# Token tile 0 first at the changes of phase, convolution inputs in 512-wide blocks, other stretches in the first feed-forward front

## The chip, the core and the metric

The kernel runs on one core of a Trainium2 chip. The metric is the device time of one execution in microseconds (us); a lower one is better. Engines are named as in the profile: PE (TensorE matmuls), PEld (its weight loads), DVE (VectorE), ACT (ScalarE), POOL (GpSimd), SP (SyncE, which issues all loads here).

## What is computed

One layer of a streaming encoder on 256 tokens of width 2048, in float32:

```python
h = modulate(rms_norm(x, g_pre[0]), sh1, sc1)
x = x + 0.5 * gt1 * rms_norm(swiglu(h, gate1, up1, down1), g_post[0])   # 5632 wide

h = modulate(rms_norm(x, g_pre[1]), sh2, sc2)
u_conv, q, k, v = split(h @ w_in)                   # 2 x 1024, 1024, 1024, 1024
v_c = (a + b_a) * sigmoid(g + b_g)                  # a, g: the halves of u_conv
y_conv = silu(layer_norm(causal depthwise conv of 31 taps(v_c) + b_dw))
y_attn = diff_attention(q, k, v)                    # 8 heads, chunk-causal, ALiBi
x = x + gt2 * rms_norm(concat(y_conv, y_attn) @ w_out, g_post[1])

h = modulate(rms_norm(x, g_pre[2]), sh3, sc3)
x = x + 0.5 * gt3 * rms_norm(swiglu(h, gate2, up2, down2), g_post[2])
```

The nine rows sh, sc, gt come from `silu(c) @ w_ada`, an 18432 x 2048 matrix that is read in 144 loads of 1 MB, one per row set m (0 to 8) and channel tile kt (0 to 15).

## The kernel before

**Products.** Each float32 product is made of three matmuls (`mm3`, lines 272 to 274): every operand is split in a high part that the PE takes at full rate and a low rest. `parts` (156 to 168) loads 1 MB of weights into one of 4 `raw` buffers, ACT casts it to `hi` (line 160), DVE subtracts to get `lo` (line 162); `hi` and `lo` have 3 buffers each. Weights that run through the array against 128 tokens give tiles of 128 tokens x 512 outputs ("M form": `m_product`, 24 matmuls of 512 columns for 1 MB). `s_tile` and the class `Front` hold the weights in the array and run 256 tokens through ("S form": 48 matmuls of 256 columns for 1 MB, result with channels on the partitions).

**Phases.** There are three: feed-forward 0, mixing, feed-forward 1 (l = 0, 1, 2). Each begins with `pre_norm`, which for each of the 16 channel tiles transposes the normalised rows of both token tiles on the PE (line 218), scales and shifts them on ACT or DVE (225, 222) and splits them (227, 228). `front_of` (558) does so two tiles ahead of the first block of products: for l = 1 the S form with 2 channel tiles of the convolution (`NF`, `SET`: 4 MB of weights), for l = 2 three M blocks (12 MB). The remaining convolution inputs, 12 MB, go through `s_tile`.

**End of a phase.** `m_last` (418) makes the last two output blocks token tile by token tile, so that `close` (253) of tile 0 runs while tile 1 is multiplied. `close` and `normed` add the residual (line 260), sum the squares (236), take a root and scale (247 on DVE, 245 on ACT). The gate is multiplied in place after the squares (line 489).

**The first front.** For l = 0 the h tiles become ready one by one, since each needs two chunks of w_ada (`ada_chunk`, line 183). `first_front` (518) therefore runs 4 fronts of 3 blocks in 4 stretches of 4 channel tiles (`CUTS`), and spills the sums between the stretches (lines 354, 358). Within a stretch the tiles of the next one are made.

**Chunks in the background.** 96 chunks of w_ada (m = 2 to 7) are drawn from the generator `bg`: in the last stretch of the first front, then one per 1.1 loads in the first feed-forward (`EVERY1`; 80 calls of `tick`), 8 in the mixing, the rest in the front of l = 2. They share the `raw` buffers and the SP queue with the weights; in the front of l = 2 their DVE work stands behind the newest `pre_norm` (`behind_dve`).

**Convolution.** When a pair of channel tiles is ready, its 62 taps (`tap`, lines 627 and 630, DVE) go to the list `fill`; each later call of `parts` puts 6 of them behind its own `lo`. What is left when half of the second `of_heads` block is done is issued at once by `conv_done` (832), and `center`, `normalize` and the products `of_conv` follow.

**Order.** A scheduler places the instructions of each engine by program order and by its own estimate of when they can run; the engines take them in that fixed order. `behind` and `behind_dve` set a lower bound for some. PSUM has 8 banks.

## Time and profile before

| | us |
|---|---|
| median of 3 runs (lowest, highest) | 1912.85 (1911.74, 1914.44) |
| the profiled execution | 1911.84 |
| its span in the trace | 1910.0 |
| PE busy in the span | 1836.3 (96%) |
| DVE busy | 1423.6 (75%) |
| ACT busy | 821.4 (43%) |
| moved by DMA | 492.58 MB, mean 258 GB/s |

A matmul's record overlaps the next one, and its end is modelled. So the busy share of the PE tells where it had nothing at all, and the distance of two starts, or the count in a stretch, tells what a matmul costs. "Idle before, <- X" names what ended the wait.

### The profile page before, as it was taken

The page shows a single profiled execution, that of the slowest core. Times are in us where ns is not written, and L with a number is a line of the kernel's source. Part 1 is how long each engine was busy: PE and PEld are TensorE (multiplying, and loading weights), DVE is VectorE, ACT ScalarE, POOL GpSimd, SP SyncE. Part 2 cuts the span into 40 slices and gives each one's busy share as a digit, 9 for nine tenths or more (in the row PEclk, how much of TensorE's full clock was granted, in tenths as well). Part 3 has the DMA queues.
Part 4 walks back from the last instruction along what each step waited for, and adds up shares of the span by engine and source line. Part 5 has one row for each costly group of instructions (what it writes and reads, how often), then busy time and mean ns, then how long its engine had stood idle before and what let it go on. Part 6 is the DMA issues. An engine that isn't in the chain of part 4 may idle for free.

```text
span 1910.0 us, 22064 instructions
## 1 busy us (share of the span) xinstructions
PE 1836.3 (96%) x8944; PEld 1542.5 (81%) x8944; DVE 1423.6 (75%) x1594; ACT 821.4 (43%) x852; POOL 6.0 (0%) x49
## 2 busy tenths in 40 slices
PE   5999999999999999799998897999999999999997
PEld 3788888888888888699997686788888888888886
DVE  7789999788889888688998967854555555555455
ACT  4544445433433334643554454544344333343342
POOL 0000000000000000000000000000000000000000
PEclk9999999999999999899999898999999999999999
DMA  9888877989999998355444665865665666565552
GB/s 362 320 317 330 337 278 290 358 345 361 357 357 370 349 367 323 122 182 185 157 174 157 242 241 202 331 238 205 236 220 205 235 220 226 215 235 210 194 193 72
DMA packets 68934, 492.58 MB, mean 258 GB/s; under 512 B 7648, under 2 KB 7776, under 8 KB 9440
## 3 DMA queue, kind: packets, MB, share of 16 engines
q1 hardware_dynamic: 68832, 491.17, 69.0%
q8 instruction: 70, 1.15, 0.2%
q14 instruction: 32, 0.26, 0.0%
HBM read 489.05 MB, written 2.10 MB: 257 GB/s over the span
## 4 chain that ended last, share of the span: by engine, by line
PE 89%; DVE 5%; ACT 3%; DMA 2%; issue 0%; SPq 0%; DVEq 0%; ACTq 0%
PE ps L273 29%; PE ps L274 29%; PE ps L272 28%; DVE lo L162 2%; DMA raw<-in_wgu 2%; ACT hi L160 1%; DVE raw L183 1%; PE ps L413 1%; ACT tmp L236 1%; PE ps L312 0%; PE ps L311 0%; DMA raw<-in_wk 0%; PE ps L313 0%; PE ps L678 0%; PE ps L218 0%
## 5 line engine op out<-in xcount | busy, mean ns | idle before, releaser
L162 DVE TENSOR_TENSOR lo<-raw,hi 128x2048 fp32r<-128x2048 f32 x314 | 718.5, 2290 | 359.8 <-ACT hi L160 359.1
L160 ACT CAST hi<-raw 128x2048 fp32r<-128x2048 f32 x314 | 600.3, 1912 | 732.4 <-PE ps L274 362.0
L272 PE MATMUL ps<-hi,big 128*128 128x512 f32 x2256 | 879.2, 395 | 16.9 <-ACT big L227 11.3
L273 PE MATMUL ps<-lo,big 128*128 128x512 f32 x2256 | 884.0, 392 | 2.8 <-DVE lo L162 2.8
L274 PE MATMUL ps<-hi,big 128*128 128x512 f32 x2256 | 881.5, 392 | 2.0 <-DVE big L175 1.2
L272 PEld LDWEIGHTS ps<-hi,big 128*128 128x128 f32 x2256 | 426.1, 189 | 106.4 <-ACT big L227 12.7
L273 PEld LDWEIGHTS ps<-lo,big 128*128 128x128 f32 x2256 | 426.5, 189 | 92.5 <-DVE lo L162 6.2
L274 PEld LDWEIGHTS ps<-hi,big 128*128 128x128 f32 x2256 | 425.7, 189 | 92.5 <-DVE big L175 2.5
L183 DVE SCALAR_TENSOR_TENSOR raw<-raw,crow 128x2048 f32<-128x2048 f32 x144 | 327.7, 2283 | 0.6 <-DMA raw<-in_wada 0.5
L272 PE MATMUL ps<-big,hi 128*128 128x256 f32 x448 | 127.3, 284 | 0.0
L273 PE MATMUL ps<-big,hi 128*128 128x256 f32 x448 | 126.7, 283 | 0.0
L274 PE MATMUL ps<-big,lo 128*128 128x256 f32 x448 | 126.7, 283 | 0.0
L630 DVE SCALAR_TENSOR_TENSOR big<-big,par,big 128x256 f32<-128x256 f32 x240 | 100.1, 477 | 0.0
L272 PEld LDWEIGHTS ps<-big,hi 128*128 128x128 f32 x448 | 85.9, 192 | 0.3 <-issue 0.3
L273 PEld LDWEIGHTS ps<-big,hi 128*128 128x128 f32 x448 | 86.0, 192 | 0.0
L274 PEld LDWEIGHTS ps<-big,lo 128*128 128x128 f32 x448 | 85.9, 192 | 0.0
L397 ACT ACTIVATE tmp<-ps 128x256 f32<-128x256 f32 x64 | 24.3, 384 | 96.3 <-PE ps L274 96.3
L486 DVE TENSOR_TENSOR big<-ps,big 128x512 f32<-128x512 f32 x48 | 32.9, 691 | 31.7 <-PE ps L274 31.7
L358 DVE TENSOR_TENSOR big<-ps,big 128x512 f32<-128x512 f32 x72 | 45.2, 681 | 5.4 <-PE ps L274 5.4
L398 DVE TENSOR_TENSOR tmp<-ps,tmp 128x256 f32<-128x256 f32 x64 | 26.1, 421 | 30.9 <-ACT tmp L397 30.9
L218 PE MATMUL ps<-ident,big 128*128 128x128 f32 x96 | 19.7, 297 | 29.6 <-DVE big L247 28.7
L173 ACT CAST big<-ps 128x512 fp32r<-128x512 f32 x44 | 25.8, 585 | 38.0 <-PE ps L413 38.0
(135 smaller groups left out, 742.6 us busy)
## 6 DMA issues: line engine op xcount, KB each, us to landing
raw<-in_wada SPq DMA_DIRECT2D x144, 1024.0 KB, 6.1
raw<-in_wgu SPq DMA_DIRECT2D x116, 1024.0 KB, 5.0
raw<-in_wd SPq DMA_DIRECT2D x88, 1024.0 KB, 5.0
raw<-in_wk SPq DMA_DIRECT2D x60, 1024.0 KB, 5.5
raw<-in_wqk SPq DMA_DIRECT2D x28, 1024.0 KB, 4.8
raw<-in_wo SPq DMA_DIRECT2D x16, 1024.0 KB, 4.8
raw<-in_wv SPq DMA_DIRECT2D x8, 1024.0 KB, 4.8
raw<-in_wkc SPq DMA_DIRECT2D x4, 1024.0 KB, 5.1
```

Source lines behind the costliest of these rows:

```text
L160: nc.scalar.copy(hi, raw)
L162: ins = nc.vector.tensor_tensor(out=lo, in0=raw, in1=hi.bitcast(F32), op=ALU.subtract)
L173: nc.scalar.copy(hi[:, :w], v[:, :w])
L183: nc.vector.scalar_tensor_tensor(out=raw, in0=raw, scalar=1.0, in1=crow, op0=ALU.mult, op1=ALU.mult, accum_out=acc)
L272: nc.tensor.matmul(o, ah, bh, start=first, stop=False)
L273: nc.tensor.matmul(o, ah, bl, start=False, stop=False)
L274: last_mm[0] = nc.tensor.matmul(o, al, bh, start=False, stop=last)
L358: nc.vector.tensor_tensor(out=a[t], in0=b[t], in1=a[t], op=ALU.add)
L397: nc.scalar.activation(v[:, o], b[t][:, :S], AF.Silu)
L398: nc.vector.tensor_tensor(out=v[:, o], in0=b[t][:, S:], in1=v[:, o], op=ALU.mult)
L486: nc.vector.tensor_tensor(out=y[t][u], in0=b, in1=y[t][u], op=ALU.add)
L630: nc.vector.scalar_tensor_tensor(out=cot(c), in0=vps[c][:, j:j + S], scalar=w, in1=cot(c), op0=ALU.mult, op1=ALU.add)
```

## The change

Four things are changed.

1. `Entry` takes the place of `front_of`. Its list of items goes over the first k0 = 12/n channel tiles (n blocks: 6 tiles for l = 1, 4 for l = 2) with token tile 0 alone, then over the same tiles with token tile 1, then over the rest with both. Two items (`LEAD`) are made inside `m_last`, `EARLY` = 3 steps before its last product. `pre_norm` takes the token tiles as an argument, and the gate is multiplied into a new tile (`yg`).
2. The convolution inputs are in M form: a front of 2 blocks (8 MB) and two `m_unit` of 4 MB. `gated` transposes the result back (8 transposes a block) and appends the taps; it is called through `left`, that is by a `pop` in a later unit.
3. `CUTS` is (2, 6, 11, 16): stretches of 2, 4, 5 and 5 channel tiles. A stretch of 2 has 6 weight blocks per front, loaded as 4 and 2 (1 MB and 0.5 MB); one of 5 has 15, loaded as 4, 4, 4, 3. There are 52 loads where there were 48, of the same 48 MB.
4. `EVERY1` is 1.05. The setup of lambda and of the distances stands ahead of the first feed-forward in the program.

```diff
-NF = (24, 2, 6)
+NF = (24, 4, 6)
-SET = (6, 2, 6)
-CUTS = (4, 8, 12, NK)
-EVERY1 = 1.1
+SET = (6, 4, 6)
+CUTS = (2, 6, 11, NK)
+EVERY1 = 1.05
+EARLY = 3
@@ pre_norm
-    def pre_norm(l, xn, h, kt):
+    def pre_norm(l, xn, h, kt, ts=(0, 1)):
-        for t in range(NT):
+        for t in ts:
@@ m_last
+                    if t == NT - 1 and u == units[-1][0] and k == n - EARLY:
+                        early()
                     m_product(banks[u][t], t, acts[k], ws[u][k], first[u] and k == 0, k == n - 1)
@@ ffn, evac
-                    nc.vector.tensor_tensor(out=y[t][u], in0=y[t][u], in1=gb[u], op=ALU.mult)
+                    yg = big()
+                    nc.vector.tensor_tensor(out=yg, in0=y[t][u], in1=gb[u], op=ALU.mult)
+                    y[t][u] = yg
@@ front_of
-        for i in range(NK + LEAD):
-            if i < NK:
-                need([(3 * l, i), (3 * l + 1, i)], late)
-                pre_norm(l, xn, h, i)
-            n_late += 1
-            while n_late >= LATE:
-                n_late -= LATE
-                behind_dve(next, late, None)
-            if i >= LEAD:
-                front.step(i - LEAD, i == LEAD, i == NK + LEAD - 1)
+    class Entry:
+            k0 = 4 * HI // self.front.n
+            self.items = [(kt, (t,)) for t in range(NT) for kt in range(k0)]
+            self.items += [(kt, (0, 1)) for kt in range(k0, NK)]
+        def early(self, xn):
+            for _ in range(LEAD):
+                behind(self.channels, xn)
+        def run(self, xn):
+            n_late = 0
+            for kt, ts in self.items:
+                self.channels(xn)
+                n_late += len(ts) / 2
+                while n_late >= LATE:
+                    n_late -= LATE
+                    behind_dve(next, self.late, None)
+                self.front.step(kt, kt == 0, kt == NK - 1, ts)
@@ convolution inputs
-            ba = s_tile(wqk[c - NF[1]], h)
-            bgg = s_tile(wqk[NC_ - 2 * NF[1] + c], h)
...
-        if c % 2:
-            fill += [lambda c=c_, j=j: tap(c, j) for j in range(KW) for c_ in (c - 1, c)]
+    def gated(cb, us):
+        ba, bg_ = bank(), bank()
+        for half, b in enumerate((ba, bg_)):
+            for j in range(2):
+                for t in range(NT):
+                    nc.tensor.transpose(b[:, j * S + t * P:j * S + (t + 1) * P],
+                                        us[t][:, half * S + j * P:half * S + (j + 1) * P], ident)
...
+        fill.extend([lambda c=c_, j=j: tap(c, j) for j in range(KW) for c_ in (2 * cb, 2 * cb + 1)])
+    def conv_block(cb, banks):
...
+        left.append(lambda: behind(gated, cb, us))
+    for cb in range(NC_ // 2):
+        if cb < front.n:
+            conv_block(cb, front.block(cb))
+        else:
+            conv_block(cb, m_unit([wcv[kq, cb] for kq in range(4)], hacts))
@@ heads
         project(w_q, hd, 0)
+        pop()
```

## Rows read from the trace of the kernel before

**Rows 1.** The page's head.
```profile
span 1910.0 us, 22064 instructions
```

**Rows 2.** Waits of PE: line, releaser, us in total, times, longest.
```profile
PE ps L218 <- DVE big L247: 28.7, 5, 10.9
```

**Rows 3.** Busy time by stretch, PE alone: bounds, length, busy (instructions), clock, DMA share, GB/s.
```profile
20.60:51.50 30.90, 23.10 (x74) 0.89 0.94 359
51.50:102.40 50.90, 49.55 (x222) 1.00 0.87 331
...
500.00:550.00 50.00, 49.22 (x219) 1.00 0.96 356
...
774.00:819.00 45.00, 32.59 (x238) 0.81 0.32 114
830.00:850.00 20.00, 20.00 (x169) 1.00 0.57 203
...
1084.00:1098.00 14.00, 7.73 (x26) 0.63 0.75 283
1149.70:1170.00 20.30, 8.60 (x34) 0.66 0.43 153
```

**Rows 4.** The page's groups of instructions: count, busy us, mean ns of one, idle before.
```profile
L272 PE MATMUL ps<-hi,big 128*128 128x512 f32 x2256 | 879.2, 395 | 16.9 <-ACT big L227 11.3
...
L272 PE MATMUL ps<-big,hi 128*128 128x256 f32 x448 | 127.3, 284 | 0.0
```

**Rows 5.** Timeline of PE at 1014 and 1035 us: start, length, operation.
```profile
1014.75 0.39 PE L272 MATMUL ps<-hi,big 128*128 128x512 f32 x1
1014.98 0.39 PE L273 MATMUL ps<-lo,big 128*128 128x512 f32 x1
...
1035.81 1.03 PE L760 MATMUL ps<-ident,tmp 128*128 128x128 f32 x8
```

**Rows 6.** Timeline around the change of phase to the mixing, DVE and PE.
```profile
769.29 2.73 DVE L260 SCALAR_TENSOR_TENSOR x<-big,ri,x 128x512 f32<-128x512 f32 x4
...
779.90 0.88 DVE L247 TENSOR_SCALAR big<-x,ri 128x512 f32<-128x512 f32 x2
...
785.90 0.88 DVE L247 TENSOR_SCALAR big<-x,ri 128x512 f32<-128x512 f32 x2
...
788.14 0.79 PE L311 MATMUL ps<-big,hi 128*128 128x256 f32 x2 [0.79 <-ACT big L227]
```

**Rows 7.** The same around the change of phase to feed-forward 1, DVE and SP.
```profile
1146.23 0.88 DVE L247 TENSOR_SCALAR big<-x,ri 128x512 f32<-128x512 f32 x2
...
1160.87 0.88 DVE L247 TENSOR_SCALAR big<-x,ri 128x512 f32<-128x512 f32 x2
...
1163.77 2.28 DVE L183 SCALAR_TENSOR_TENSOR raw<-raw,crow 128x2048 f32<-128x2048 f32 x1
...
1151.76 0.33 SPq L153 DMA_DIRECT2D raw<-in_wk  x1
```

**Rows 8.** Timeline of ACT at the start: first and fourth cast of weights.
```profile
17.49 1.90 ACT L160 CAST hi<-raw 128x2048 fp32r<-128x2048 f32 x1 [2.22 <-DMA raw<-in_wk]
...
46.29 1.89 ACT L160 CAST hi<-raw 128x2048 fp32r<-128x2048 f32 x1
```

**Rows 9.** Timeline of DVE and PE from the last taps to the first convolution product.
```profile
1055.63 2.06 DVE L630 SCALAR_TENSOR_TENSOR big<-big,par,big 128x256 f32<-128x256 f32 x5
1057.61 0.68 DVE L789 TENSOR_TENSOR tmp<-big,big 128x512 f32<-128x512 f32 x1
1058.22 2.28 DVE L183 SCALAR_TENSOR_TENSOR raw<-raw,crow 128x2048 f32<-128x2048 f32 x1
...
1079.53 2.28 DVE L183 SCALAR_TENSOR_TENSOR raw<-raw,crow 128x2048 f32<-128x2048 f32 x1
...
1090.73 0.80 PE L272 MATMUL ps<-hi,big 128*128 128x512 f32 x1 [3.43 <-ACT big L173]
```

**Rows 10.** DMA issues: count, KB each, median us to landing.
```profile
raw<-in_wk SPq DMA_DIRECT2D x60, 1024.0 KB, 5.5
...
x<-in_x SPq DMA_DIRECT2D x4, 512.0 KB, 6.0
```

More of the change, by code (lines that the diff above doesn't have):

```diff
@@ L48, with chunks @@
 FF_GROUPS = [(0, 12), (12, 24), (24, 36), (36, 44)]
-NF = (24, 2, 6)
+NF = (24, 4, 6)
 HM, HC, HV = 4, 3, 2
-SET = (6, 2, 6)
-CUTS = (4, 8, 12, NK)
-EVERY1 = 1.1
+SET = (6, 4, 6)
+CUTS = (2, 6, 11, NK)
+def chunks(l):
+    n = SET[l] // 2
+    r = []
+    for k0, k1 in zip((0,) + CUTS, CUTS) if l == 0 else ((0, NK),):
+        r += [(i, min(i + 4, k1 * n)) for i in range(k0 * n, k1 * n, 4)]
+    return r
+EVERY1 = 1.05
 TAPS = (3, 3, 3, 3)
@@ L218, in pre_norm @@
             nc.tensor.transpose(b[:, t * P:(t + 1) * P], src[:, o:o + P], ident)
+        if len(h) == kt:
+            h.append(big(F32R))
+        both = h[kt]
+        o, e = ts[0] * P, (ts[-1] + 1) * P
         v = tmp()
@@ L342, in step @@
                 i = kt * n + j
-                if i % 4 == 0:
-                    self.parts = quarters(self.w[i // 4])
-                for t in range(NT):
-                    m_product(self.banks[j][t], t, (self.h[kt][:, :S], self.h[kt][:, S:]), self.parts[i % 4],
-                              first, last)
+                c, i0, i1 = self.chunk[i]
+                if c not in self.parts:
+                    self.parts[c] = quarters(self.w[c], i1 - i0)
+                for t in ts:
+                    m_product(self.banks[j][t], t, (self.h[kt][:, :S], self.h[kt][:, S:]),
+                              self.parts[c][i - i0], first, last)
         def spill(self):
@@ L416, in to_acts, with m_last @@
         acts.extend([(mh[:, o:o + S], ml[:, o:o + S]) for o in (0, S)])
-    def m_last(units, acts, after):
+    def m_last(units, acts, after, early=lambda: None):
         ws, first = {}, {}
@@ L502, in ffn @@
                     gb[u] = gate_row(l, u)
-                m_last([(u, srcs(u), None) for u in range(4 - N_LAST, 4)], acts, evac)
+                m_last([(u, srcs(u), None) for u in range(4 - N_LAST, 4)], acts, evac,
+                       (lambda: nxt.early(xn)) if nxt else (lambda: None))
         return xn
@@ L521, in first_front @@
         h = []
-        front = [MFront(w, h, SET[0] // 2) for w in wk]
+        front = [Front(0, w, h) for w in wk]
         def channels(kt):
@@ L612, in block_kernel @@
     nc.vector.tensor_scalar(out=nlam, in0=nlam, scalar1=-LAM_INIT, scalar2=None, op0=ALU.add)
-    h = []
+    mixing = Entry(1, wkc[0], bg)
+    xn = ffn(0, h, None, facts, wgu1, wd1, bg, EVERY1, mixing)
     need([(m, kt) for m in (3, 4) for kt in range(NK)], bg)
-    h, front = front_of(1, xn, wkc[0], iter(()))
+    mixing.late = iter(())
+    h, front = mixing.run(xn)
     co = [big() for _ in range(NC_ // 2)]
@@ L718, in values @@
     def values(u, hooks):
-        hacts = [(h[kt][:, :S], h[kt][:, S:]) for kt in range(NK)]
         banks = m_unit([wv[kq, u] for kq in range(4)], hacts, hooks)
@@ L842, in block_kernel @@
     gb = {}
+    second = Entry(2, wk2[0], bg)
     def mix_evac(u, t, b):
@@ L861, in block_kernel @@
                 mix_evac(u, t, open_[u][t])
-    m_last([(u, of_conv(u), open_[u]) for u in range(4 - N_LAST, 4)], conv_acts, mix_evac)
-    h, front = front_of(2, xn, wk2[0], bg)
-    ffn(2, h, front, {}, wgu2, wd2, ada_of([(8, kt) for kt in range(NK)]), 6, True)
+    m_last([(u, of_conv(u), open_[u]) for u in range(4 - N_LAST, 4)], conv_acts, mix_evac,
+           lambda: second.early(xn))
+    h, front = second.run(xn)
+    ffn(2, h, front, {}, wgu2, wd2, ada_of([(8, kt) for kt in range(NK)]), 6, None)
 def _layout(i):
```

152 lines of the change are left out of this document (65 added, 87 removed).

## The prediction

> **What bounds the kernel now.** I read the head of the page first [rows 1]: the span is 1910.0 us, the profiled execution took 1911.84 us, so 1.84 us lie outside the span, and the median of the runs is 1.0 us above that execution. My sum is made against 1911.84.
>
> Next I asked what a matmul costs. The page's groups give a mean of 395 ns for 512 columns and 284 ns for 256 [rows 4]. Those are lengths of overlapping records. Two starts in a dense stretch are 0.227 us apart [rows 5], and 169 matmuls of 256 columns fill 20.0 us [rows 3], so 0.118 us each. I use these two steps. The PE is the engine that sets the time almost everywhere, and what a change can win is either fewer steps or the stretches where the PE has nothing. The stretches by time show four such places [rows 3], and the list of waits names the largest cause: transposes of `pre_norm` that wait for `normed`, 28.7 us in five waits [rows 2].
>
> - Start: from 20.6 to 51.5 us there are 74 matmuls, which are worth 74 x 0.227 = 16.8 us. So by 51.5 us 51.5 - 16.8 = 34.7 us are lost, and DMA is at 0.94. From 51.5 to 102.4 us, 222 x 0.227 = 50.4 of 50.9 us are used.
> - Entry to the mixing, 774 to 819 us: 238 instructions, of which 32 are transposes. A group of 8 transposes takes 1.03 us [rows 5], so 0.13 each. The rest is worth 206 x 0.118 + 32 x 0.13 = 28.5 us. The loss is 16.5 us. The mean clock is 0.81.
> - Entry to feed-forward 1, 1149.7 to 1170 us: 28 x 0.227 + 6 x 0.13 = 7.1 of 20.3 us. The loss is 13.2 us.
> - First convolution products, 1084 to 1098 us: 26 instructions at clock 0.63, so at least 14 - 26 x 0.227 = 8.1 us are lost.
>
> **The change part by part.** *Token tile 0 first.* Six channel tiles x 2 blocks x 3 matmuls, and four x 3 x 3, are 36 matmuls of tile 0 in each entry, 36 x 0.227 = 8.2 us of work that no longer waits for tile 1. In the entry to the mixing `normed` of tile 0 starts at 779.9 and that of tile 1 at 785.9 [rows 6]. From `normed` to the first product it is 788.1 - 785.9 = 2.2 us. With these times tile 0 could begin at 782.1 and fill 6.0 us. But tile 0 is late here: from its `close` at 769.3 to its `normed` are 10.6 us [rows 6], since splits of weights and steps of tile 1 stand between on DVE and ACT. The new tile `yg` takes one wait out of that chain. If tile 0 is ready when the last product ends (about 774 us), all 8.2 us fit. The PE also stays at the upper of its two clock levels for longer: mean 0.81 over 45 us is 17 us at half, of which about 12 are idle, so 5 us of work run at half the pace and cost 2.5 us. Against this stand the two early `pre_norm`: their transposes sit in the PE's fixed order ahead of 9 products of the old phase. If `normed` of tile 0 comes at 779.9 as before, those 9 products and the chain of tile 1 behind them wait up to 6 us. Range of the gain 2 to 10.7; I take 7.
>
> In the entry to feed-forward 1, `normed` of tile 0 starts at 1146.2, ahead of the last product, and that of tile 1 at 1160.9 [rows 7]. So the early transposes hold nothing back. Here the weights could: the third chunk of the front is issued only at 1151.8, because three chunks of w_ada hold `raw` buffers until their DVE step, the first at 1163.8 [rows 7]. In the new order only one chunk of w_ada stands ahead of that load (`n_late` counts halves), so the load moves forward into the old phase and ACT and DVE can split it as soon as `hi` is free. Gain 8.2 us and part of the clock loss, less 1 to 2 us by which the extra halves of `pre_norm` hold up the chain of tile 1. Range 4 to 11; I take 9.
>
> *Convolution inputs in M form.* 16 MB change form: 48 x 0.118 = 5.68 us each before, 24 x 0.227 = 5.44 us after, so 16 x 0.24 = 3.8 us less. The way back costs 32 transposes, 32 x 0.13 = 4.1 us. Together 0. (The mean lengths would have given 16 x (48 x 0.284 - 24 x 0.395) = 66 us, which is not there.) The Trainium skill, "TensorE: Matmul & The Clock Gate", section "Back-to-back issue gap", puts a matmul at N/2.4 + 2.5 ns, 109 ns for 256 columns and 216 ns for 512. By that, an estimate, the form would win only 16 x (5.24 - 5.18) = 1 us and lose 3 us with the transposes. The rows differ from it by 9 and 11 ns, and I go by the rows.
>
> *Taps.* This is the price of the new form. Before, `fill` has entries after the first pair, and 12 convolution loads, 16 of q and k, 8 of v and 4 of the heads take 6 each: 240 of 248 taps, and 8 are left for `conv_done`. After, the front's 8 loads take none, since `gated` comes only with the `pop` in the next unit, after that unit's first load. So 3 + 4 + 16 + 8 + 4 = 35 loads take 210 taps and 38 are left. Five taps and the step to the next operation take 1.98 us [rows 9], 0.396 each, so 30 more are 11.9 us of DVE between the last load and `center`. The first convolution product hangs on that chain: last tap to 1057.6, `center` from there, product at 1090.7 [rows 9], and the PE waits for it. Not all of 11.9 us need show. Between 1058.2 and 1079.5 four passes over w_ada, 2.28 us each [rows 9], stand in the chain's gaps, 9.1 us that can come later. Upward, two `lo` of the next unit, which read as many elements (2 x 2.3), and these passes may end up ahead of the chain: 11.9 + 4.6 + 9.1 = 25. Range 3 to 25. I take 8, nearer the lower end, since `center` finished well before its sum on the PE was due.
>
> *Stretches.* In the first stretch 6 channels (12 loads of w_ada) and 6 MB of weights are moved, 18 MB. The stretch to 51.5 us moved 359 GB/s, 2.92 us for 1 MB [rows 3]. The third load was cast at 17.5 us and the twelfth at 46.3 [rows 8], 3.2 us each. At 3.0 us the last one is there at 17.4 + 15 x 3.0 = 62.4, and with 2.4 us for its split and 2.7 us for its 12 products the stretch ends at 67.5 us. Its products are 4 x 6 x 2 x 3 x 0.227 = 32.7 us, so 34.8 us are lost, where before 34.7 were lost at 51.5 us. The first h comes no sooner in either. So 0. Bounds: loads of 0.5 MB may cost as much as whole ones (512 KB landed in 6.0 us, 1024 KB in 5.5 [rows 10]); four of them at 1.5 us extra are +6. If the two chunks of the last channel come after the weights of the stretch, it ends 2 x 3.0 us sooner, less a little that the next stretch waits: -5. Later stretches are set by the PE.
>
> *Background.* 80 calls at 1.05 give 76 chunks instead of 72, and the last front stretch gives 6 instead of 5. So feed-forward 0 moves 4 MB more, 11.7 us of DMA time where DMA is at 0.96 and 0.8 us of 50 are idle [rows 3]. As the PE was just covered there, I take +1.5, up to +8. The front of l = 2 moves 5 MB less: 6 instead of 11 chunks, -1 (0 to -1.5). The split of `pre_norm` adds no PE work. `yg`, the earlier setup, the odd loads of 0.75 MB lie beside products: 0, and if uncovered one load's 3 us.
>
> Sum: -7 - 9 + 0 + 8 + 0 + 1.5 - 1 = -7.5, so 1911.84 - 7.5 = 1904.3 us. I forecast 1904.
>
> **Rivals.**
> - *The tail of taps is absorbed.* The scheduler puts the passes over w_ada behind the chain, 11.9 - 9.1 = 3, and both entries give their full amounts: -10 - 10 + 3 + 0.5 = -16.5, 1895 us. For it: PE idles in the chain anyway. Against: the PE takes the two sums of the layer norm at fixed places.
> - *Tile 0 does not lead.* `normed` of tile 0 comes as late as before and the early transposes block the PE: 2 + 4 won, 8 lost, 0.5: +2.5, 1914 us, no change that can be measured. For it: 779.9 against 774 in the first entry. Against: 1146.2 against 1149.7 in the second.
> - *The tail of taps takes over the stage.* At `conv_done`, 38 taps stand ahead of `center` and of the next `lo`, and the chain comes the full 25 us late: -16 + 25 + 0.5 = +9.5, 1921 us. It turns the sign once the first convolution product comes more than about 20 us later against the end of the old phase than the 316 us of now (774 to 1090). For it: 30 taps are certain by the count. Against: half of the 25 us are passes that nothing needs yet.
>
> **How the numbers follow.** Forecast (1897 to 1909) 0.48, absorbed tail 0.18, no lead 0.18, tail takes over 0.16. About 0.2%, 3.8 us, is what a measurement of this kernel can tell from no change, so "same" is 1909.0 to 1916.7. Faster 0.48 + 0.18 = 0.66, same 0.18, slower 0.16. The range takes in the absorbed tail with the better bound of the start (1890) and reaches towards the taking over of the tail (1918): 1889 to 1918.
>
> **What would show it.** In the trace after, tile 0's products should start within 3 us of the last product of the old phase, and the 28.7 us of waits on `normed` should fall under 12. The convolution loads should be 24 matmuls 0.227 apart. About 38 taps should stand between the last `lo` ahead of `conv_done` and `center`, which begins some 12 us later against that `lo`. The clock should stay up through the entries. 5 loads fewer of w_ada should lie in the front of l = 2. I would be wrong if the early transposes show as a PE wait in front of the last 9 products, if the PE waits in the last 20 us of the mixing grow by over 15 us, or if the start loses over 40 us.

## The result: slower by 1.1%

| | us |
|---|---|
| median before, 4 runs beside the changed kernel | 1913.14 (1911.74 to 1914.44) |
| median after, 4 runs | 1934.17 (1931.64 to 1934.83) |
| ratio, 95% interval | 1.0108 (1.0090 to 1.0125) |
| profiled execution after, its span | 1931.64, 1929.8 |
| forecast, range | 1904, 1889 to 1918 |

The forecast had the wrong sign and the time lies above its range. The head of the page after, the line of PE, and the shares of the engines on the chain that ended last (PE had 89% of that chain before, DVE 5%, DMA 2%):

```profile
span 1929.8 us, 21442 instructions
...
PE 1843.6 (96%) x8592; PEld 1524.7 (79%) x8592; DVE 1425.5 (74%) x1613; ACT 828.5 (43%) x879; POOL 6.0 (0%) x49
...
PE 77%; DVE 11%; DMA 7%; ACT 4%; issue 1%; SPq 0%; DVEq 0%; ACTq 0%
```

PE still has 96%, and that share says nothing: what changed is how much of the chain goes through the other engines.

**Where the time went.** I followed the PE through both traces by the distance from each matmul's start to the next, less what a matmul costs in a dense stretch (0.2267 us for 512 columns, 0.1183 for 256, 0.109 for a transpose). What is left over is a loss, whatever its cause, a low clock included. The work, counted at these steps, is the same in both kernels, 1803.1 us before and 1802.8 after. The losses from the first to the last matmul are 92.8 and 113.9 us, 21.1 more, against 19.8 us more of span. Their places, in us, for all kernels of this study (times without a number of runs are one run each):

| | start, to 150 us | FF 0, 150 to 700 | its end | entry 1 | mixing | tail of the convolution | entry 2 | front of l = 2 | from 1880 us | time (runs) |
|---|---|---|---|---|---|---|---|---|---|---|
| before | 31.8 | 3.2 | 0.2 | 17.0 | 3.6 | 20.1 | 14.2 | 2.0 | 0.0 | 1913.14 (4) |
| after | 39.9 | 8.8 | 4.6 | 12.8 | 2.7 | 32.5 | 9.9 | 0.5 | 1.5 | 1934.17 (4) |
| e1 | 33.9 | 7.7 | 4.6 | 12.9 | 2.6 | 28.4 | 8.9 | 3.2 | 1.5 | 1921.83 |
| e2 | 42.5 | 5.8 | 2.7 | 15.2 | 2.6 | 32.3 | 9.8 | 4.7 | 1.5 | 1935.59 |
| e3 | 42.1 | 9.3 | 4.9 | 15.5 | 3.6 | 16.9 | 8.9 | 1.1 | 1.5 | 1922.25 |
| e4 | 43.3 | 8.2 | 4.7 | 16.3 | 2.6 | 32.6 | 14.8 | 0.4 | 1.6 | 1943.00 |
| e5 | 32.5 | 8.0 | 0.2 | 16.4 | 3.7 | 29.4 | 14.4 | 2.7 | 0.0 | 1927.12 |
| e6 | 32.5 | 3.2 | 3.4 | 15.5 | 3.4 | 21.4 | 9.7 | 7.2 | 1.5 | 1914.48 (12) |
| e7 | 33.3 | 6.2 | 3.9 | 12.8 | 3.5 | 21.3 | 9.4 | 3.2 | 1.5 | 1917.39 (12) |
| e8 | 44.3 | 9.4 | 4.1 | 15.4 | 2.7 | 32.4 | 9.8 | 0.7 | 1.6 | 1938.84 |
| e9 | 34.2 | 2.3 | 0.3 | 14.1 | 3.4 | 21.1 | 9.7 | 6.6 | 0.0 | 1910.55 (11) |
| e11 | 37.2 | 15.7 | 6.7 | 12.8 | 2.7 | 32.4 | 9.9 | 0.5 | 1.6 | 1937.77 |
| e12 | 38.8 | 5.8 | 0.3 | 14.8 | 3.4 | 16.9 | 9.0 | 16.2 | 0.0 | 1925.79 (4) |
| e13 | 35.2 | 4.4 | 0.2 | 14.9 | 3.5 | 21.2 | 9.6 | 3.2 | 0.0 | 1912.92 (11) |

The entries are counted from 12 us (l = 1) or 4 us (l = 2) ahead of their first transposes to 32 and 36 us behind them, the tail 45 us to both sides of the first sum of the layer norm. Each row is one trace. Kernels with the same program up to 150 us (after, e2, e3, e4) differ by up to 3.4 us there. The kernel before and e5 run the same instructions in the same order up to 819 us, and lose 3.2 and 8.0 us in feed-forward 0. The changed kernel and e3 do so up to 861 us, and lose 12.8 and 15.5 us in entry 1. So a single difference of 3 us in the first column or in entry 1, or of 5 us in feed-forward 0, says little.

Four places got worse: the start by 8.1, the first feed-forward with its end by 10.0, the tail of the convolution by 12.4, the end of the kernel by 1.5. The entries got better by 4.2 and 4.3.

**The tail, after.** Waits of PE between 1040 and 1130 us (line, releaser, us in total, times, longest), then what the DVE does ahead of the first sum:

```profile
PE ps L806 <- DVE tmp L814: 11.4, 1, 11.4
PE ps L286 <- ACT big L185: 5.3, 1, 5.3
```

```profile
1066.52 2.27 DVE L174 TENSOR_TENSOR lo<-raw,hi 128x2048 fp32r<-128x2048 f32 x1
1068.72 17.50 DVE L633 SCALAR_TENSOR_TENSOR big<-big,par,big 128x256 f32<-128x256 f32 x44
1086.15 0.67 DVE L812 TENSOR_TENSOR tmp<-big,big 128x512 f32<-128x512 f32 x1
1086.76 2.27 DVE L174 TENSOR_TENSOR lo<-raw,hi 128x2048 fp32r<-128x2048 f32 x1
1088.96 0.67 DVE L814 TENSOR_TENSOR tmp<-tmp,big 128x512 f32<-128x512 f32 x1
1089.56 2.27 DVE L174 TENSOR_TENSOR lo<-raw,hi 128x2048 fp32r<-128x2048 f32 x1
1091.76 0.67 DVE L814 TENSOR_TENSOR tmp<-tmp,big 128x512 f32<-128x512 f32 x1
...
1094.57 2.27 DVE L195 SCALAR_TENSOR_TENSOR raw<-raw,crow 128x2048 f32<-128x2048 f32 x1
```

44 taps stand in one block: the last 6 that `parts` takes and the 38 that are left. `center` (line 812) comes behind them, where before it came right behind 5 taps [rows 9]. Two `lo` got in between its additions, which end at 1092.4 us, and the first sum on the PE waits 11.4 us for that. Two passes over w_ada (the second at 1094.57) come behind the additions, ahead of the subtractions of `center`. Before, the additions ended at 1061.8 us and the sum started at 1068.5 without a wait, so there were 6.7 us of room. Against the PE's own work the additions now end 18 us later: 11.9 us are the 30 taps. Most of the rest are three `lo` of 2.27 us ahead of and between the additions, where before one pass over w_ada of 2.28 us stood.

**The end of the first feed-forward, after.** ACT, PE and SP around 767 us, in this order:

```profile
766.11 0.63 ACT L250 ACTIVATE tmp<-big 128x512 f32<-128x512 f32 x1 [8.57 <-DVE big L467]
...
767.41 1.64 ACT L185 CAST big<-raw 128x512 fp32r<-128x512 f32 x3
...
768.07 0.50 PE L286 MATMUL ps<-big,big 128*128 128x512 f32 x1 [2.04 <-ACT big L185]
...
753.21 10.00 SPq L165 DMA_DIRECT2D raw<-in_wd  x4
773.21 0.93 SPq L165 DMA_DIRECT2D raw<-in_wkc  x2
```

The casts of the second-last block's weights into `big` tiles (line 185) begin at 767.41 us, although those weights were issued from 753.21 us on. In ACT's fixed order they stand behind the squares of the block before (line 250), for which ACT has waited 8.57 us. The PE waits for the first cast. The loads of the convolution inputs (`in_wkc`) need the `raw` buffers and are issued only at 773.21 us, when the subtraction behind the first casts (line 187) is done.

**The start, after.** Busy time by stretch (bounds, length, PE, PEld, DVE, ACT, POOL, clock, DMA share, GB/s), and DVE in the middle of the second stretch:

```profile
60.00:80.00 20.00, 15.32 (x64) 11.61 (x65) 15.33 (x13) 12.55 (x17) 0.00 (x0) 1.00 0.79 303
110.00:130.00 20.00, 17.18 (x78) 13.76 (x77) 20.00 (x24) 10.51 (x9) 0.00 (x0) 1.00 0.89 347
```

```profile
118.55 2.29 DVE L195 SCALAR_TENSOR_TENSOR raw<-raw,crow 128x2048 f32<-128x2048 f32 x1
...
120.76 2.29 DVE L195 SCALAR_TENSOR_TENSOR raw<-raw,crow 128x2048 f32<-128x2048 f32 x1
...
122.97 3.72 DVE L337 TENSOR_TENSOR big<-ps,big 128x512 f32<-128x512 f32 x6
...
126.81 2.28 DVE L174 TENSOR_TENSOR lo<-raw,hi 128x2048 fp32r<-128x2048 f32 x1
```

Two passes over w_ada and six additions of sums stand in a row ahead of the next `lo`, and in 20 us the DVE has no gap at all. The loss between 60 and 80 us is of another kind: the DVE has gaps there, and the PE waits 3.4 us for casts of weights on ACT and 1.7 us for `lo`. Between 500 and 550 us 215 matmuls run instead of the 219 of [rows 3].

**The entries, after.** DVE and PE at the first:

```profile
787.60 2.74 DVE L274 SCALAR_TENSOR_TENSOR x<-big,ri,x 128x512 f32<-128x512 f32 x4
...
791.67 2.29 DVE L174 TENSOR_TENSOR lo<-raw,hi 128x2048 fp32r<-128x2048 f32 x1 [1.32 <-ACT hi L172]
...
797.70 0.88 DVE L261 TENSOR_SCALAR big<-x,ri 128x512 f32<-128x512 f32 x2
...
800.80 0.49 DVE L243 TENSOR_TENSOR big<-tmp,big 128x128 fp32r<-128x128 f32 x2
...
807.95 0.49 DVE L243 TENSOR_TENSOR big<-tmp,big 128x128 fp32r<-128x128 f32 x2 [0.67 <-ACT big L242]
...
791.82 0.39 PE L288 MATMUL ps<-hi,big 128*128 128x512 f32 x1
798.24 0.90 PE L230 MATMUL ps<-ident,big 128*128 128x128 f32 x3 [6.04 <-DVE big L261]
800.34 0.80 PE L286 MATMUL ps<-hi,big 128*128 128x512 f32 x1 [1.19 <-ACT big L242]
```

From `close` of tile 0 to its `normed` are still 10.1 us (10.6 in [rows 6]): two `lo` of 2.29 us stand in the chain, at 791.67 and 795.30. So tile 0 leads, but from 800.34 us, 8.5 us behind the start of the last product of the old phase. And only 12 of its 36 matmuls run before the PE waits again (1.9 us) for tile 1: its first two h tiles are split at 800.80 (line 243), the next ones at 807.95, behind the `close` of tile 1 (from 801.82). At the second entry tile 0 leads at once (DVE, then PE):

```profile
1171.50 0.88 DVE L261 TENSOR_SCALAR big<-x,ri 128x512 f32<-128x512 f32 x2
...
1176.91 0.49 DVE L243 TENSOR_TENSOR big<-tmp,big 128x128 fp32r<-128x128 f32 x2
...
1181.29 2.74 DVE L274 SCALAR_TENSOR_TENSOR x<-big,ri,x 128x512 f32<-128x512 f32 x4
...
1187.20 0.49 DVE L243 TENSOR_TENSOR big<-tmp,big 128x128 fp32r<-128x128 f32 x2
...
1173.25 0.38 PE L230 MATMUL ps<-ident,big 128*128 128x128 f32 x2
...
1175.31 0.40 PE L288 MATMUL ps<-hi,big 128*128 128x512 f32 x1
...
1175.57 0.47 PE L286 MATMUL ps<-hi,big 128*128 128x512 f32 x1
...
1179.88 0.39 PE L288 MATMUL ps<-hi,big 128*128 128x512 f32 x1
...
1186.18 0.90 PE L230 MATMUL ps<-ident,big 128*128 128x128 f32 x3 [5.92 <-DVE big L261]
```

The early transposes (1173.25) stand ahead of the last 9 products of the old phase, which end with the one at 1175.31, and hold nothing up; the new phase starts at 1175.57. At 1180 us the products of the two h tiles that are ready are used up, 18 of the 36 matmuls of tile 0, and the PE waits 5.9 us for tile 1. The next h tiles are split only at 1187.20, behind the `close` of tile 1 (1181.29).

### The profile page after: what moved, and what is told of

It is laid out like the page before. It is cut to its first block, busy times and chain, and to the rows that moved or that the text cites. A ratio compares the mean times of both kernels' runs of the same rounds, so it can differ in the third digit from the quotient of the medians.

```text
span 1929.8 us, 21442 instructions
## 1 busy us (share of the span) xinstructions
PE 1843.6 (96%) x8592; PEld 1524.7 (79%) x8592; DVE 1425.5 (74%) x1613; ACT 828.5 (43%) x879; POOL 6.0 (0%) x49
## 4 chain that ended last, share of the span: by engine, by line
PE 77%; DVE 11%; DMA 7%; ACT 4%; issue 1%; SPq 0%; DVEq 0%; ACTq 0%
PE ps L287 25%; PE ps L288 25%; PE ps L286 25%; DVE lo L174 5%; DMA raw<-in_wgu 4%; DVE raw L195 3%; ACT hi L172 3%; DMA raw<-in_wd 2%; DVE big L633 1%; PE ps L392 1%; DVE big L337 1%; ACT tmp L250 1%; DVE big L467 0%; DMA raw<-in_wk 0%; PE ps L701 0%
## 5 line engine op out<-in xcount | busy, mean ns | idle before, releaser
L174 DVE TENSOR_TENSOR lo<-raw,hi 128x2048 fp32r<-128x2048 f32 (+2 forms) x318 | 718.8, 2263 | 379.6 <-ACT hi L172 379.3
L286 PE MATMUL ps<-hi,big 128*128 128x512 f32 x2384 | 927.7, 397 | 23.4 <-ACT hi L172 10.7
L287 PE MATMUL ps<-lo,big 128*128 128x512 f32 x2384 | 937.7, 393 | 9.5 <-DVE lo L174 9.1
L288 PE MATMUL ps<-hi,big 128*128 128x512 f32 x2384 | 932.0, 392 | 1.4 <-DVE big L187 1.4
L172 ACT CAST hi<-raw 128x2048 fp32r<-128x2048 f32 (+2 forms) x318 | 600.9, 1891 | 761.6 <-PE ps L288 387.3
L286 PEld LDWEIGHTS ps<-hi,big 128*128 128x128 f32 x2384 | 451.7, 190 | 119.1 <-ACT hi L172 11.8
L287 PEld LDWEIGHTS ps<-lo,big 128*128 128x128 f32 x2384 | 451.6, 189 | 109.8 <-DVE lo L174 19.0
L288 PEld LDWEIGHTS ps<-hi,big 128*128 128x128 f32 x2384 | 450.0, 189 | 97.0 <-DVE big L187 2.9
L286 PE MATMUL ps<-big,hi 128*128 128x256 f32 x256 | 73.1, 285 | 0.0
L287 PE MATMUL ps<-big,hi 128*128 128x256 f32 x256 | 72.4, 283 | 0.0
L288 PE MATMUL ps<-big,lo 128*128 128x256 f32 x256 | 72.4, 283 | 0.0
L286 PEld LDWEIGHTS ps<-big,hi 128*128 128x128 f32 x256 | 49.1, 192 | 0.4 <-issue 0.3
L287 PEld LDWEIGHTS ps<-big,hi 128*128 128x128 f32 x256 | 49.1, 192 | 0.0
L288 PEld LDWEIGHTS ps<-big,lo 128*128 128x128 f32 x256 | 49.1, 192 | 0.0
L467 DVE TENSOR_TENSOR big<-ps,big 128x512 f32<-128x512 f32 x48 | 32.5, 689 | 21.4 <-PE ps L288 21.2
L185 ACT CAST big<-ps 128x512 fp32r<-128x512 f32 x44 | 25.7, 584 | 35.2 <-PE ps L392 35.2
```

The source lines that it names most:

```text
L172: nc.scalar.copy(hi[:, :w], raw[:, :w])
L174: ins = nc.vector.tensor_tensor(out=lo[:, :w], in0=raw[:, :w], in1=hi[:, :w].bitcast(F32), op=ALU.subtract)
L185: nc.scalar.copy(hi[:, :w], v[:, :w])
L286: nc.tensor.matmul(o, ah, bh, start=first, stop=False)
L287: nc.tensor.matmul(o, ah, bl, start=False, stop=False)
L288: last_mm[0] = nc.tensor.matmul(o, al, bh, start=False, stop=last)
```

## Experiments

Kernels e1 to e4 and e8 are the changed kernel with one part undone or altered. e5 is the kernel before with one part of the change put in. e6, e7, e9 and e13 are steps towards a version without the losses. e11 and e12 try the stretches.

### e1: stretches of 4 again

```diff
-CUTS = (2, 6, 11, NK)
+CUTS = (4, 8, 12, NK)
```

> The changed kernel with the stretches of before (4, 8, 12, 16), all else as changed. Theory: the PE loses 8 us more than before up to 150 us of the trace, and the stretches of 2, 4, 5, 5 are the whole cause; with 4, 4, 4, 4 this falls from about 40 to about 32 us, the time from 1934 to about 1926. Rival: the start is slower because other work (the setup ahead of the first feed-forward, the faster background) stands there too; then the loss to 150 us stays above 37 us and the time within 3 us of 1934.

Measured: 1921.83 us, one run, 12.3 under the median of the changed kernel and 9.8 under the execution whose losses the table has. The start loses 33.9 us instead of 39.9, and the stretches of the start are full again; the same two stretches as above:

```profile
60.00:80.00 20.00, 20.00 (x92) 16.44 (x91) 13.95 (x12) 11.86 (x14) 0.00 (x0) 1.00 0.88 340
110.00:130.00 20.00, 20.00 (x90) 16.38 (x89) 18.64 (x18) 7.64 (x6) 0.00 (x0) 1.00 0.78 292
```

The theory holds: the stretches cost 6 us at the start. The rest of the gain lies in the tail (4.1) and in the first feed-forward (1.1), which this edit does not touch; the table shows where, not why.

### e2: a chunk per 1.1 loads again

```diff
-EVERY1 = 1.05
+EVERY1 = 1.1
```

> The changed kernel with one background chunk per 1.1 loads, as before. Theory: in the first feed-forward DMA was just covered by the PE, and 4 MB more let the PE wait, 8 us between 440 and 720 us and 4 us for the weights of the last two blocks at 765 us; with 1.1 these 12 us fall to about 3, the time to about 1925. Rival: the chunk that the longer last stretch adds and the later start shift the weights, and the rate is no cause; then the waits there stay above 8 us and the time within 3 us of 1934.

Measured: 1935.59 us. The first feed-forward gives back 3.0 us and its end 1.9, and the front of l = 2 takes 4.2, where the PE waits 3.3 us for `lo` in two waits. The theory (12 us down to 3, a time of 1925) fell; the rival (within 3 us of 1934) held: in this run the rate alone moves a loss of 3 to 5 us from one place to another.

### e3: 8 taps behind each load of the convolution, q and k (an entry of `TAPS` counts pairs)

```diff
-TAPS = (3, 3, 3, 3)
+TAPS = (4, 3, 3, 3)
```

> The changed kernel with 8 taps behind each load of the convolution and of q and k instead of 6, so that none are left at the end. Theory: the 44 taps in a row ahead of the layer norm's first sum hold the convolution products back; the PE's losses from the heads' blocks to those products fall from 32 to about 17 us, of which 0 to 8 us come back in the q and k stage, where DVE was 95% busy; time 1917 to 1926. Rival: the tail is late for another reason (the sums' places on the PE, the passes over w_ada); then the losses there stay above 28 us.

Measured: 1922.25 us, 11.9 under the median and 9.4 under the profiled execution. The tail loses 16.9 us instead of 32.5. The wait on `center` (11.4 us) is gone and that on the casts (5.3) is halved; the longest that is left is one on the attention, which the kernel before has too (5.8 us). Waits of PE between 1035 and 1125 us:

```profile
PE ps L782 <- DVE tmp L772: 7.4, 1, 7.4
PE ps L286 <- ACT big L185: 2.5, 1, 2.5
```

The backlog of taps is the cause of the tail's loss. Part of the 15.6 us is the clock: e3 and e12 are at 16.9, and e6, e7, e9 and e13, with the same taps, at 21.1 to 21.4. From about 20 us behind the first sum the granted clock stands at 0.50 for 3.4 us in e3 and e12 and for 10.2 us in those four and in the kernel before, and the casts wait 2.5 us (e3) instead of 3.4 (before). So the backlog is worth 11 to 15.6 us here.

### e4: both tiles together at the entries

```diff
-            self.items = [(kt, (t,)) for t in range(NT) for kt in range(k0)]
-            self.items += [(kt, (0, 1)) for kt in range(k0, NK)]
+            self.items = [(kt, (0, 1)) for kt in range(NK)]
@@ early
-            for _ in range(LEAD):
-                behind(self.channels, xn)
+            pass
@@ run
+            for _ in range(LEAD):
+                self.channels(xn)
+                n_late += 1
```

> The changed kernel without the lead of token tile 0: each item of the entries has both tiles, two items are made ahead after the old phase, none inside it. Theory: the lead wins 10 us in the two entries (their losses are 12 and 9.5 us with it, 17 and 16 before); without it they rise to about 33 us together and the time to about 1944. Rival: the entries are shorter because of the M form and the new tile for the gate, not of the lead; then the time stays within 3 us of 1934.

Measured: 1943.00 us, 8.8 over the median. The entries lose 16.3 and 14.8 us, 8.4 more than the changed kernel's together. Waits of PE on `normed` at the two entries, in this order; in the changed kernel they are 7.9 and 5.9 us:

```profile
PE ps L230 <- DVE big L261: 12.1, 2, 6.1
...
PE ps L230 <- DVE big L261: 11.0, 1, 11.0
```

The theory (10 us) holds in kind. At the second entry the lead is worth 4.9 us. At the first it is 3.5 us against the changed kernel, but 0.8 against e3. That one has the lead too, and its waits there are as long (7.6 us on `normed`, 7.9 in the changed kernel), but in e3 the granted clock stands at 0.50 for 10.2 us and then for 3.4 more, in the changed kernel for 6.8. So 6 to 8 us for both, about half of what was forecast.

### e5: the kernel before, with 38 taps left

```diff
+    skip = [5]
@@ parts
-        if fill:
+        if fill and skip[0]:
+            skip[0] -= 1
+        elif fill:
```

> The kernel before, where the first five loads after the first pair of channel tiles take no taps, so that 38 instead of 8 are left at the end: the changed kernel's tail alone. Theory: the block of taps on DVE ahead of the layer norm is the price; the losses ahead of the convolution products rise from 20 to 31 to 34 us, the time by 11 to 14 us to about 1925. Rival: the chain has room and the M form is what makes it late; then the time rises by less than 5 us.

Measured: 1927.12 us beside 1914.34, the median of the kernel before. The tail loses 29.4 us, 9.3 more than before, with the same block of taps on the DVE, and the same wait of the first sum on the PE, 11.7 us. The block in the timeline:

```profile
1061.12 17.52 DVE L633 SCALAR_TENSOR_TENSOR big<-big,par,big 128x256 f32<-128x256 f32 x44
```

Together with e3 the tail is settled from both sides: the backlog makes 9.3 of its 12.4 us in S form too, and the same long wait. This trace also loses 4.8 us more in the first feed-forward, 4.3 of its 8.0 us between 540 and 555 us (1.1 before), for which I have no cause: no tap is due there, and the order of instructions is that of the kernel before. So that much can differ between executions.

### e6 and e7: the parts undone together

```diff
-CUTS = (2, 6, 11, NK)
+CUTS = (4, 8, 12, NK)
-TAPS = (3, 3, 3, 3)
+TAPS = (4, 3, 3, 3)
@@ e6 alone
-EVERY1 = 1.05
+EVERY1 = 1.1
```

> The changed kernel with stretches of 4, one background chunk per 1.1 loads, and 8 taps per load in the convolution, q and k: what is left of the change is the lead of token tile 0 and the M form. Theory (the three losses are independent and the lead is worth 9 us): PE losses 32 to 34 up to 150 us, about 5 in the first feed-forward, 28 in the two entries, 17 ahead of the convolution products, 84 to 88 in all against 93 before; time 1904 to 1909, ratio to before 0.995 to 0.998. Rival (the losses replace one another, as the rate of the background did): total above 92, time within 4 us of before.

> As the kernel with three undone, but with the changed rate of 1.05 in the background. Theory: the rate moves about 5 us of waiting from the front of the second feed-forward into the first feed-forward and is worth nothing: the same time within 2 us. Rival: the waits in the first feed-forward are late weights that the rate causes; then this one is 4 to 8 us slower than the one with three undone.

Measured, beside 1914.34 for the kernel before: e6 1914.48 us, ratio 1.0004 (0.9994 to 1.0014); e7 1917.39 us, ratio 1.0019 (1.0008 to 1.0031). Start and tail are back to the values of the kernel before within 1.5 us, the entries keep 6.0 (e6) and 9.0 us (e7; the 2.7 between them are the clock at the first entry, as under e4), and still the time is no better. The theory for e6 fell and its rival held, the losses being above 92 us. e7 is 2.9 us slower than e6, between its theory (2) and its rival (4 to 8). The table shows what eats it: 3.2 to 3.7 us at the end of the first feed-forward and 1.5 at the end of the kernel, both of which the kernel before hasn't, and 5.2 us in the front of l = 2 (e6) or 3.0 and 1.2 us in the two feed-forward places (e7).

### e8: small loads filled up to 1 MB

```diff
-        nc.sync.dma_start(raw[:, :w], src)
+        nc.sync.dma_start(raw, src)
@@ quarters
-        w = parts(src[:, :n * 512], n * 512)
+        w = parts(src, n * 512)
```

> The changed kernel, where the loads of 0.5 and 0.75 MB move a whole 1 MB (the rest is zeros that nobody reads). Theory: at the start a raw buffer and its turn are what counts, not the bytes, so that a half load costs as much as a whole one: losses up to 150 us within 2 us of the changed kernel's 40 to 43. Rival: bytes count; four half loads more are 2 MB, 6 us more loss in the first stretch.

Measured: 1938.84 us; the start loses 44.3 us, where the changed kernel and those with the same start lost 39.9 to 43.3. Up to 150 us the changed kernel has five small loads, and the four of 512 KB land no sooner than whole ones (count, KB each, median us from issue to landing):

```profile
raw<-in_wk SPq DMA_DIRECT2D x19, 1024.0 KB, 6.2
raw<-in_wk SPq DMA_DIRECT2D x4, 512.0 KB, 6.3
```

Filled up they move 2.25 MB more, 6.6 us of DMA time at the 2.92 us that the prediction has for 1 MB, and cost 1.0 to 4.4 us. The spread of equal starts is as large, so this run decides little: the small loads neither cost like whole ones for certain, nor by their bytes.

### e9: e6 with the gate in place

```diff
-                    yg = big()
-                    nc.vector.tensor_tensor(out=yg, in0=y[t][u], in1=gb[u], op=ALU.mult)
-                    y[t][u] = yg
+                    nc.vector.tensor_tensor(out=y[t][u], in0=y[t][u], in1=gb[u], op=ALU.mult)
```

> e6 (stretches of 4, a chunk per 1.1 loads, a first pair of 4) with one thing more undone: the gate is multiplied into the rows in place, as in the kernel before, and not into a new tile of the 43 big buffers. Theory (the new tile holds buffers that the casts of the second-last block's weights wait for): the first of these casts in the first feed-forward, 30 us before the last product in the kernel before and 24 to 30 in e6, comes early again; the PE loses 0.2 us between 700 us and the first entry instead of 3.4, and about 1.4 us less in the last 10 us, and the time falls by 3 to 5 us to 1910 (ratio to before 0.998, 0.997 to 0.999). Rival A (the new tile shortens the chain to the normalised rows, because the squares no longer have to be done before the gate writes): the waits come down as in the theory, but the normalised rows come later and the entries lose 1 to 4 us more than 15.5 and 15.1; time as e6, 1914. Rival B (the wait comes from the 2 early items in the last block, not from the tile): losses before the entry stay at 3.4, time 1914.

Measured: 1910.55 us beside 1913.97, ratio 0.9980 (0.9971 to 0.9989), and 3.9 under e6. Its ACT and SP around the end of the first feed-forward, to be read beside the casts at 767.41 and the loads at 773.21 us above (this kernel ends the phase at 775.5 us, the changed one at 791.8):

```profile
746.00 2.19 ACT L185 CAST big<-raw 128x512 fp32r<-128x512 f32 x4 [1.80 <-DMA raw<-in_wd]
...
740.04 9.48 SPq L165 DMA_DIRECT2D raw<-in_wd  x4
751.67 13.44 SPq L165 DMA_DIRECT2D raw<-in_wkc  x5
```

The kernel that differs from it by the tile alone is e6, and its casts start here:

```profile
754.19 1.12 ACT L185 CAST big<-raw 128x512 fp32r<-128x512 f32 x2
```

In e9 the casts follow their loads again, the first 29.5 us ahead of the start of the last product, where e6 has 23.3 and the changed kernel 24.4. The loads of the next phase are issued 23.8 us ahead of it, where e6 has 18.1 and the changed kernel 18.6. The losses at the end of the feed-forward (3.4) and of the kernel (1.5) are gone. Rival A, that the entries lose more in return, fell: they lose 23.8 us, 1.4 less than in e6. Rival B, the early items, fell too: they are in both kernels. The tile `yg` is the cause. Whether it acts by holding a buffer that the casts need, or by the place that the planned order gives them, stays open: a larger number of `big` buffers wasn't tried.

### e11: stretches of 2, 4, 4, 6

```diff
-CUTS = (2, 6, 11, NK)
+CUTS = (2, 6, 10, NK)
```

> The changed kernel with stretches of 2, 4, 4, 6 in place of 2, 4, 5, 5. Theory (in the second stretch, 16 steps, 5 channel tiles are made, 10 loads of w_ada, and the DVE is full there): with 4 tiles in the second stretch the 5.1 us that the PE loses between 111 and 150 us go to under 1, and the third stretch, now 6 tiles in 16 steps, loses them instead, 5 to 8 us between 150 and 210 us, where the changed kernel loses none; time within 3 us of the changed kernel, 1931 to 1937. Rival (the loss comes from the smaller loads and the order of the loads at the start, not from how many tiles are made per step): 111 to 150 us keeps its 5, and nothing new is lost between 150 and 210; time 1934.

Measured: 1937.77 us. The stretch that makes five channel tiles in the changed kernel makes four here and loses nothing, and the one that makes six loses 8.9 us between 163 and 222 us. Its stretches:

```profile
110.00:130.00 20.00, 20.00 (x91) 16.55 (x90) 18.93 (x20) 8.47 (x6) 0.00 (x0) 1.00 0.85 330
...
165.00:185.00 20.00, 17.78 (x73) 14.10 (x72) 20.00 (x21) 6.08 (x7) 0.00 (x0) 0.91 0.92 358
200.00:222.00 22.00, 19.66 (x81) 15.39 (x80) 22.00 (x25) 8.27 (x8) 0.00 (x0) 0.93 0.87 330
```

From 100 us on, PE loses where the DVE has no gap, and that goes with the tiles per step: 4 in 16 steps fit (here) and 5 in 20 (third stretch of the changed kernel), 5 and 6 in 16 do not. The loss between 60 and 80 us stays as it was (7.6 us).

### e12: e9 with five stretches

```diff
-CUTS = (4, 8, 12, NK)
+CUTS = (2, 6, 10, 14, NK)
```

> e9 with 5 stretches of 2, 4, 4, 4, 2: the short first stretch of the change with no later stretch that makes more than 4 channel tiles in 16 steps, and 24 more additions of sums on the DVE (some 15 us of it by the rows of spill, 0.62 us each). If the gain of the short first stretch is real (in the changed kernel the PE lost 28 us up to 59 us, 31.5 in the kernel with stretches of 4, up to there) and the later loss comes from the tiles made per step alone, the PE loses 28 to 30 us up to 150 us instead of 32.5, and the time is 2 to 4 us under that of e9, 1906 to 1908. Rival (the short first stretch itself makes the losses between 59 and 76 us, because 4 tiles are made in its 6 steps): 34 to 37 us lost up to 150 us, time 2 to 4 us over e9, 1912 to 1915.

Measured: 1925.79 us, ratio 1.0066 (1.0051 to 1.0082). The start loses 38.8 us, more than even the rival said, again between 59 and 80 us, where 4 tiles are made in the 6 steps of the first stretch. All seven kernels with a first stretch of 2 lose 6.7 to 7.8 us there, the seven with a first stretch of 4 lose 0.1. So the short first stretch has a price that no division of the rest takes away; whether the tiles per step make it was not tried apart. The front of l = 2 loses 16.2 us, which neither theory had: the last front stretch of 8 steps draws 2 chunks of w_ada instead of 5, by its steps in the code, so three more are left for that front (14 loads of w_ada in the trace, 11 in e9); that they make the wait was not tried apart. The longest wait of PE there is one of 8.0 us on the cast of a weight load.

### e13: e9 with a chunk per 1.05 loads

```diff
-EVERY1 = 1.1
+EVERY1 = 1.05
```

> e9 with a chunk of w_ada per 1.05 loads in place of 1.1. Theory (with the gate in place the first feed-forward has its buffers back, so the 5 more chunks it takes cost it nothing, and the front of l = 2 keeps the 3 to 6 us that it loses for them between 1194 and 1225 us in e9): losses between 150 and 700 us under 3.5, from 1194 to 1225 us under 2 instead of 6.2; time 2 to 5 us under e9, 1906 to 1908, ratio to before 0.996. Rival (the rate makes the short waits on the lo parts in the first feed-forward whatever the buffers, 6.2 us between 150 and 700 us in e7 against 3.2 in e6): the two cancel, 1910 to 1913, ratio 0.998 to 1.000.

Measured: 1912.92 us beside 1912.56, ratio 1.0001 (0.9992 to 1.0010). The front of l = 2 gains 3.4 us and the first feed-forward loses 2.1; the rival was right in the time. The faster rate wins nothing, and by the medians it costs 2.4 us here (the ratios of e9 and e13 to the kernel before lie apart, each with its interval) and 2.9 us from e6 to e7. e9 is the only kernel here that is faster than the one before, by 0.2%. Its profiled trace does not show that gain: its losses are 92.8 us, as many as in the trace of before, and of the 3.4 us between the medians the profiled executions (1911.05 and 1911.84) show 0.8.

## Why the prediction was wrong, step by step

From the forecast of 1904.3 us to the profiled execution of 1931.64 are 27.3 us. By the table of this one execution they come from four terms: background and `yg` +10.0 (5.6 + 4.4 + 1.5 measured, 1.5 forecast), stretches +8.1, entries +7.5, taps +4.4. The rest makes -2.7: the PE's work, the mixing, the front of l = 2, and 1.0 us less from the last matmul to the end of the span.

- **Entries: right in kind, mis-sized.** I took -7 and -9; they gave -4.2 and -4.3 in this trace, inside the bounds of both (2 to 10.7, 4 to 11), at their lower ends. The term that was mis-sized is the 36 matmuls of tile 0 in each entry, "8.2 us of work that no longer waits for tile 1". Before the wait for tile 1 the trace has 12 of them in the first entry and 18 in the second, 2.7 and 4.1 us. I counted what does not need tile 1, not what is ready: only two of its h tiles are, since ACT and DVE do the `close` and `normed` of tile 1 ahead of the next ones. In the first entry another step failed too, "tile 0 is ready when the last product ends". I had written down the 10.6 us from its `close` to its `normed`, with the splits of weights in between, and then let them go because one wait left the chain; they were 10.1 us after. In the second the chain of tile 1 is 14.1 us behind tile 0 (14.6 before, [rows 7]), and the PE waits 5.9 us of it. Each wait that is left keeps its part of the clock loss, which I had counted as gained. That the first gain lies inside its bounds is luck: with the clock of e3 (15.5 us lost) it is 1.5 us. The early transposes did not hold up the last 9 products, which was the rival "tile 0 does not lead".
- **Form: right.** The PE's work is 0.3 us less, against 0 forecast. By the figures of the Trainium skill that the prediction cites there it would have been 3 us more, and the rows at 0.227 us were the better ground. That section of the Trainium skill gives them for a matmul in isolation, and not for a stream with a weight load for each matmul, which is what runs here.
- **Taps: right in the count and in the mechanism, mis-sized.** 38 taps were left, as counted, and 44 of them stand in a row. I took +8 of a range of 3 to 25; it was +12.4 after and +9.3 in e5. "`center` finished well before its sum on the PE was due" was true (6.7 us of room) and still no reason to go to the lower end: the additions came 18 us later against the PE, because of the taps and of `lo` ahead of and between them, as the upper bound said, and the PE has nothing else to do at that place. The two passes over w_ada cost the second part of `center`, not the wait for the first sum. The mark that I had set for this rival (a first product 20 us later against the end of the old phase) was badly chosen: it came at 1114.64 us, 322.8 us behind the start of the last product of the old phase, where the kernel before has 317.0, because the entry's gain lies in the same span of time.
- **Stretches: failed.** I took 0, with bounds of -5 and +6; it was +8.1. The end of the first stretch was costed with care, and came 3.3 us later than that: at 70.8 us instead of 67.5, with 38.1 us lost by the prediction's count instead of 34.8. Up to 59 us less is lost than before (28.0 against 29.5), then 6.7 up to 80 us, part of it behind the end of the stretch, and 5.2 from 100 to 150, where the kernel before loses 0.3. The step that failed is the last sentence, "Later stretches are set by the PE". It rested on the rows of a kernel with 4 tiles in 16 steps [rows 3], and the change has 4 tiles in 6 steps and 5 in 16. With stretches of 4 the DVE has 1.4 us of gap in 20 (the row of e1 at 110 us), by estimate some 4.4 us in the 65 us that 16 steps of 18 matmuls take; one pass over w_ada takes 2.29 us, so the two of one more tile use it up. e11 moves that loss along with the tiles, e1 takes it away. What makes the loss between 60 and 80 us beyond the short first stretch stays open.
- **Background: mis-sized, and its neighbour failed.** +1.5 (to +8) was given for 4 MB more; the rate measures 3.0 (e2 against the changed kernel), 3.0 (e6, e7) and 2.1 us (e9, e13): three times the same sign, each less than the 4.8 us by which equal programs differ there. The rest of the 5.6 us has no cause shown. The front of l = 2 gave 1.5 back (1 forecast), with 6 loads of w_ada left for it instead of 11, as counted. What failed is "`yg` ... lie beside products: 0". It costs 3 to 4 us at the end of the first feed-forward and 1.5 at the end of the kernel, by e6 and e9 and by the order of casts and squares in the trace. I had looked at what the tile takes out of the chain (a wait) and not at what it does to the casts far ahead of it.

Of the rivals "the tail of taps takes over the stage" came nearest: it has the sign and the wait right, but the tail is +12.4 and not +25, and the time is 13 us above its 1921. No rival had the losses of the stretches and of `yg`.

The signs named in the prediction, in one place: waits on `normed` went from 28.7 to 20.0 us, not under 12 (6.1 of them stand at the very start of the kernel and could not go). Products within 3 us held in the second entry, not in the first. The clock stayed up over more of the first entry in this execution, 0.92 over the 45 us that answer to the 0.81 of [rows 3]. The start lost 39.9 us, at the mark.

A rule of the Trainium skill comes near to the loss by `yg`: "Perfetto Trace Analysis", section "Optimization Strategy", reads the same gap repeating on the engine that should be saturated as a sign that there may not be enough SBUF or PSUM for the next tile. The gap here is not repeated, it comes once at each end of a feed-forward, and that a buffer was missing is not shown, so this trace shows a case beside the rule rather than one of it.

## What to carry to other kernels

A work list that an engine empties in passing (the taps behind each load) has a due time: count how many loads are left once the list can fill, and raise what each takes before moving its start. Check every engine, not only the one that sets the time, against the new number of steps a stretch has for the same work: the DVE with 1.4 us of gap in 20 had no room here for two more passes of 2.29 us in 16 steps. A lead is worth the work that is ready before the wait, not all the work that does not need the late operand: count what the other engines have finished by then. And a new tile is not free because its operation is: it changes what the scheduler places where, perhaps by the buffer that it takes, and casts far ahead of it may be what comes late.

## What the runs showed of the hardware

After the 6.0 us wait of the first entry the matmuls of the changed kernel start 0.43 us apart, at a granted clock of 0.50, until about 803 us, and 0.23 us apart where the clock is back. The busy time by stretch, with the clock behind the engines; the third row is e3 as far behind its wait as the second is in the changed kernel:

```profile
801.00:803.00 2.00, 2.00 (x6) 1.44 (x5) 1.70 (x6) 0.60 (x2) 0.12 (x1) 0.50 0.35 147
803.00:805.00 2.00, 2.00 (x10) 1.46 (x8) 1.88 (x4) 2.00 (x7) 0.12 (x1) 0.92 0.00 0
...
806.00:808.00 2.00, 2.00 (x6) 1.53 (x5) 1.90 (x4) 2.00 (x7) 0.25 (x2) 0.50 0.00 0
```

For nearly 3 us the work is done at half the pace here, at 1.2 instead of 2.4 GHz, and the lead of tile 0 is spent in just that time: the products that were to fill the wait run at the lower level, because the wait in front of them is still there. I had not expected that a shorter wait would keep this part of its cost. Nor is that part fixed: in e3 the instructions and their order are the same and the waits nearly so (7.6 us on `normed` instead of 7.9), but the clock is back only 3 us later and falls once more, and the entry loses 2.7 us more.
